# Expert weights in blocks of 1024 columns, down rows two to a partition, one low-part operation a load, and a fixed ring of five stages

## The chip, the cores and the metric

The kernel runs on one core of one Trainium2 chip. The metric is the device time of one execution in microseconds (us), the median of several runs. The engines are TensorE (PE; its weight loads are listed apart as PEld), VectorE (DVE), ScalarE (ACT), GpSimd (POOL) and SyncE (SP), whose queue issues the transfers from HBM.

## What is computed

A transformer with 256 tokens of 1024 features in float32: a first block of two layers (differential attention with a dense feed-forward, then a gated recurrence with a mixture of experts) and a second block of two layers (sparse attention with a gated MLP, a feed-forward with a short convolution, and a gated projection). The part that the change is about is the mixture of experts:

```python
logits = (t @ w_router).astype(F32)
top_val, top_idx = lax.top_k(logits, 2)                  # of 8 experts
combine = ...                                            # softmax of the two, by expert
for e in range(8):
    gt, up = jnp.split(t @ w_gate_up[e], 2, axis=-1)     # 1024 -> 2 * 3584
    y = (jax.nn.silu(gt) * up) @ w_down[e]               # 3584 -> 1024
    out = out + combine[:, e:e + 1] * y
```

The weights of the eight experts are 8 x 3 x 1024 x 3584 floats, 352 MB. Each is read once.

## The kernel before, in words

**Float32 products.** PE multiplies in a reduced format (float32r). Each operand is therefore split into a high part (a rounded copy, made by ACT, line 229) and a low part (the rest, a subtraction on DVE, line 230), and each product is three matmuls: high by high, low by high, high by low. Every weight tile of the program takes the same way: SP issues a load into a *stage* (`wload`, L217; pool `stp`, `N_STAGE` = 5 tiles of 128 x 2048 floats, 1 MB); ACT writes the high part and DVE the low part, in two halves of 128 x 1024 (`wsplit`, pools `whp` with `N_HI` = 6 halves and `wlp` with `N_LO` = 5); PE reads both; then stage and halves are free again. ACT and DVE work in order, so an instruction that waits holds up those behind it.

**Who sets the order.** The program is written with tile pools under `TileContext(nc, auto_bufs=True)`. A planner places the instructions of each engine at build time, by dependences, free buffers and its own estimates of cost. It may take a later instruction first, and it may raise the number of buffers of a pool where its walk gets stuck. On the chip each engine then follows its list. The order that the trace shows is therefore not always that of the source.

**The experts** (`moe`, `expert`, `run_experts`). The tokens of two experts at a time are gathered by matmul (`pair`), up to 128 tokens each; a branch handles the case of more than 128 and is not taken here. For each expert, seven groups of 512 hidden columns: `gate_up(g)` multiplies the tokens with the gate columns and the up columns (`pg`, `pu`, two PSUM banks of pool `pb`; four loads of 4 feature blocks x 512 columns, named `ste`, whose parts are `hie` and `loe`; 48 matmuls, L264 to L266), then ACT applies silu (L1137) and DVE multiplies (L1138), which gives `eh`. `down(g)` turns `eh` by four transposes (L1146), splits it (`hh` on ACT L283, `hl` on DVE L284) and multiplies with two loads of 256 rows of the down weights (`std`, with `hid` and `lod`; 24 matmuls of 512 columns, L1158 high by high, L1159 low by high, L1160 high by low), summed in two banks `y` over the seven groups. The loop runs `gate_up(g)` and then `down(g - 1)`. `scatter` brings `y` back to the tokens. One such round of 72 matmuls and six loads is called a *group* below, and the passage from the last matmul of `gate_up` to the first products of `down` a *turn*; there are 56 of each.

**The feed-forwards** (`swiglu_ff`, once in the first block, twice in the second) go through 11 *pairs* of 128 hidden columns: a gate tile `g` and an up tile `u` (8 feature blocks x 256 columns, `hig`/`log` and `hiu`/`lou`), 96 matmuls of 256 columns in the order of the feature blocks, so that both tiles are read to the end; then `down` of the pair before (a tile `dn`, 48 matmuls). DVE takes the sums out of PSUM (L640), ACT and DVE do the rest and split the result.

Of the kernel before, what the change touches and what calls it, by code (L numbers as in the profile page):

```python
# [10 lines left out]
F32 = mybir.dt.float32  # L11
# [11 lines left out]
N_AHEAD = (2, 0)  # L23
# [6 lines left out]
N_STAGE, N_HI, N_LO, N_G, N_T, N_S = 5, 6, 5, 30, 14, 64  # L30
# [64 lines left out]
# vectors over the features, as columns of 128: (key, how many columns)  # L95
# [15 lines left out]
def layout(v):  # L111
    """the arrays of the launch: the weights as they come, the rest laid out as the chip reads it"""
# [21 lines left out]
def body(ctx: ExitStack, tc: tile.TileContext, I, out, stop=None):  # L134
# [4 lines left out]
    stp = ctx.enter_context(tc.tile_pool(name="stp", bufs=N_STAGE))  # L139
# [27 lines left out]
    def S(n, s="s"):  # L167
        return sp.tile([128, 16 if n <= 16 else 64], F32, tag="s" if n <= 16 else "sw", name=nm(s), bufs=N_S if n <= 16 else 1)[:, :n]
# [16 lines left out]
    keep = {F32: cst.tile([128, 4096], F32, name="keep"), F32R: cst.tile([128, 512], F32R, name="keepr")}  # L185
# [12 lines left out]
    V.memset(onec, 1.0 / 1024)  # L198

# [7 lines left out]
    class Halves:  # L207
        def __init__(self, tiles, per):
            self.tiles, self.per = tiles, per

        def __getitem__(self, idx):
            _, k, sl = idx
            return self.tiles[k // self.per][:, k % self.per, sl]

    def wload(w, k0, kn, c0, width, s):
        st = stp.tile([128, 2048], F32, tag="st", name=nm("st" + s))
        nc.sync.dma_start(r3(st[:, :kn * width], kn),  # L217
                          w[k0 * 128:(k0 + kn) * 128, c0:c0 + width].rearrange("(k p) f -> p k f", p=128))
        return st, kn, kn * width, s

    def wsplit(loaded):
        st, kn, n, s = loaded
        his, los = [], []
        m = n // 2
        for q in range(2):
            hi = whp.tile([128, 1024], F32R, tag="hi", name=nm("hi" + s))
            lo = wlp.tile([128, 1024], F32R, tag="lo", name=nm("lo" + s))
            sq = st[:, q * m:q * m + m]
            A.activation(hi[:, :m], sq, AF.Copy)  # L229
            V.tensor_tensor(lo[:, :m], sq, hi.bitcast(F32)[:, :m], op=OP.subtract)  # L230
            his.append(r3(hi[:, :m], kn // 2))
            los.append(r3(lo[:, :m], kn // 2))
        return Halves(his, kn // 2), Halves(los, kn // 2)

    def wtile(w, k0, kn, c0, width, s):
        return wsplit(wload(w, k0, kn, c0, width, s))

# [8 lines left out]
    def wpieces(w, k0, kn, c0, width, s):  # L246
        """wtile in pieces of 512, which leaves its tiles to what is under way"""
        wh, wl = Pieces(), Pieces()
        for k in range(kn):
            for f in range(width // 512):  # L250
                st, hi, lo = G("st" + s), G2("hi" + s, F32R), G("lo" + s, F32R)
                nc.sync.dma_start(st, w[(k0 + k) * 128:(k0 + k) * 128 + 128, c0 + f * 512:c0 + f * 512 + 512])
                split(st, hi, lo, None)
                wh.tiles[k, f], wl.tiles[k, f] = hi, lo
        return wh, wl
# [74 lines left out]
    def squares(src, how):  # L330
        """tiles whose sum over features, through the matrix of ones, is the mean square"""
# [10 lines left out]
    def stats_r(src, how="later"):  # L342
        """1 / rms over the 1024 features, by token"""
# [13 lines left out]
    def rows_R(r, keep=True):  # L357
        """the same along the free dimension"""
# [48 lines left out]
    def feat_1024(X, w, s, order, side=None, hook=None):  # L407
        """X times w, by features; side yields what it makes of X while the rest is multiplied"""
# [67 lines left out]
    def steps(gen, n=None):  # L476
        """runs n steps of a generator (all of them without n); whether it goes on"""
# [42 lines left out]
    def by_R(lst, R, f=None, tile=G):  # L520
        """keeps a product by features, times R"""
# [9 lines left out]
    def by_r(lst, r, func=AF.Copy, tile=G):  # L531
        """keeps a product by tokens, times r"""
# [12 lines left out]
    def mem_attn(qmT, kmT, vm, XC):  # L545
        """attention over the memory (queries scaled), its output in pair 3 of XC"""
# [44 lines left out]
    def head_rms(po, extra, XC, hp, col):  # L591
        """rms norm of two heads by token and (times extra), then their transposes, split"""
# [398 lines left out]
    def moe(acc):  # L991
        # the first weights, before the branch
        ahead = []
        for n in range(N_AHEAD[0]):
            g, kh, b = n // 4, n // 2 % 2, n % 2
            ld = wload(I["moe_w_gate_up"][0, 0], kh * 4, 4, b * 3584 + g * 512, 512, "e")
            if n < N_AHEAD[1]:
                ahead.append(lambda hl=wsplit(ld): hl)
            else:
                ahead.append(lambda ld=ld: wsplit(ld))  # L1000
# [17 lines left out]
        # tokens by rows, split  # L1018
# [47 lines left out]
        # the rms of the tokens, and the weights of their two experts  # L1066
# [56 lines left out]
        def expert(e, X, j, SC, cw, first):  # L1123
            wgu, wd = I["moe_w_gate_up"][0, e], I["moe_w_down"][0, e]
            load = wtile if first else wpieces
            y = []

            def gate_up(g):
                pg, pu = PB("pg"), PB("pu")
                for kh in range(2):  # L1130
                    for ps, c0 in ((pg, g * 512), (pu, 3584 + g * 512)):
                        wh, wl = ahead.pop(0)() if ahead and first else load(wgu, kh * 4, 4, c0, 512, "e")
                        for k in range(4):
                            mm3t(ps, X, kh * 4 + k, j, wh[:, k, :], wl[:, k, :], kh == 0 and k == 0, kh == 1 and k == 3)
                t = G2("eh")
                rc = cw[:, 2 * j + 1:2 * j + 2]
                A.activation(t, pg, AF.Silu, scale=rc)  # L1137
                V.scalar_tensor_tensor(t, pu, rc, t, op0=OP.mult, op1=OP.mult)  # L1138
                return t

            def down(g, t):
                if g == 0:
                    y.extend([PA("y"), PA("y")])
                pt = PC("ht")
                for f in range(4):
                    T.transpose(pt[:, f * 128:f * 128 + 128], t[:, f * 128:f * 128 + 128], ident)  # L1146
                h, l = G2("hh", F32R), G2("hl", F32R)
                split(pt, h, l, None)
                for fp in range(2):
                    wh, wl = load(wd, g * 4 + fp * 2, 2, 0, 1024, "d")  # L1150
                    order = [(f, hf) for f in range(2) for hf in range(2)]
                    if g == 6 and fp == 1:
                        order = [(f, hf) for hf in range(2) for f in range(2)]
                    for f, hf in order:
                        fs = slice((fp * 2 + f) * 128, (fp * 2 + f) * 128 + 128)
                        a, b = wh[:, f, hf * 512:hf * 512 + 512], wl[:, f, hf * 512:hf * 512 + 512]
                        opens, ends = g == 0 and fp == 0 and f == 0, g == 6 and fp == 1 and f == 1
                        T.matmul(y[hf], lhsT=h[:, fs], rhs=a, start=opens, stop=False)  # L1158
                        T.matmul(y[hf], lhsT=l[:, fs], rhs=a, start=False, stop=False)  # L1159
                        T.matmul(y[hf], lhsT=h[:, fs], rhs=b, start=False, stop=ends)  # L1160
# [18 lines left out]
        def run_experts(slot, first):  # L1179
            ctxs = {0: pair(0, slot)}  # L1180
            prev = None
            fns = {}
            for e in range(8):
                for g in range(7):
# [5 lines left out]
                    if prev is not None:  # L1190
                        pe, pg, pt = prev
                        fns[pe][1](pg, pt)
                        if pg == 6:
                            fns[pe][2]()
                    prev = (e, g, t)
                    if first and e % 2 == 1 and g == 3 and e < 7:
                        ctxs[e // 2 + 1] = pair(e // 2 + 1, slot)
            fns[7][1](6, prev[2])
# [27 lines left out]
    def post(acc, gain, cols, fill):  # L1226
        """adds the normalized acc; the operand of the next products comes with it"""
# [18 lines left out]
    def proj(i, out):  # L1246
        """p @ w_ple_proj, features by rows, halved (the gate's own half lies in tanh)"""
# [19 lines left out]
    def gelu_gen(x, n):  # L1267
        """x (1 + tanh(...)) in place: twice the gelu"""
# [8 lines left out]
    def second_loads(i):  # L1277
        load_cols(I["cols2"][i], COLS_2, str(i), [("w2", 256)])
        if i == 0:
            k2 = cst.tile([128, sum(OFFS[n][1] for n in K2)], F32, name="k2")  # L1280
# [10 lines left out]
    def second(i, pj, fill, X):  # L1291
# [117 lines left out]
        # keys and values  # L1409
# [14 lines left out]
        # queries, their two parts side by side  # L1424
# [52 lines left out]
        gts = [sp.tile([128, 24], F32, tag="gates", name=nm("gates"), bufs=2) for _ in range(2)]  # L1477
# [90 lines left out]
        facs = [sp.tile([128, 24], F32, tag="fac", name=nm("fac"), bufs=2) for _ in range(2)]  # L1568

        def cmp_attn(c):  # L1570
            """over the compressed keys: opens at[c]"""
# [266 lines left out]
```

## Time and profile before

| | |
|---|---|
| median of 3 runs | 2308.17 us (2307.86 to 2312.56) |
| profiled execution, its own time | 2313.2 us, which is the span of the profile; nothing lies around it |
| instructions in it | 36939 |
| read from HBM | 547.70 MB |

The profile is of one execution, on the one core that is used. Busy time on PE is modelled: a matmul stays busy until its result has drained, so that neighbours overlap, and the pace of PE is read from the starts of its matmuls. PEclk is the granted clock of TensorE as a share of 2.4 GHz. A wait is put down to the instruction that released it.

### The profile page before, as it was taken

To read this page: it belongs to the slowest core of one execution; us is meant where nothing else is said; L and a number is where in the kernel's file an instruction comes from. 1 tells how busy PE (TensorE), PEld (TensorE's weight loads), DVE (VectorE), ACT (ScalarE), POOL (GpSimd) and SP (SyncE) were. 2 spreads that over 40 slices of the span, in tenths; PEclk is the share of its full clock that TensorE was granted. 3 is DMA by queue.
4 is the path that set the end of the run, shared out by engine and by line. 5 is a ranking of instruction groups with operands and counts; after the bars stand their busy time and mean duration, and the time that the engine had idled before them with its cause. 6 is when DMAs were issued, how large, how long until landed. Compare 5 with 4: busy or idle time off the path is not lost. (4 is left out here: it accounts for less than half of the span.)

```text
span 2313.2 us, 36939 instructions
## 1 busy us (share of the span) xinstructions
PE 2239.2 (97%) x14218; PEld 2019.2 (87%) x14218; DVE 1817.8 (79%) x2701; ACT 1474.7 (64%) x2138; POOL 76.4 (3%) x83
## 2 busy tenths in 40 slices
PE   8999999998999999999999999999999999989998
PEld 7889999997878888888888888879899998989998
DVE  6666576766888898989898989888777777867776
ACT  5554457435777777777777777777665565765554
POOL 0100001000000000000000000000000001000001
PEclk9999999998999999999999999999999999989998
DMA  8445556224999999999999999986245544525550
GB/s 288 139 137 174 195 171 204 92 78 167 359 348 335 349 353 372 338 354 351 373 350 341 349 378 350 372 299 221 74 136 193 182 147 137 186 78 183 183 178 19
DMA packets 297113, 551.23 MB, mean 238 GB/s; under 512 B 10336, under 2 KB 132064, under 8 KB 296928
## 3 DMA queue, kind: packets, MB, share of 16 engines
q1 hardware_dynamic: 296928, 548.78, 67.5%
q8 instruction: 114, 1.87, 0.3%
q14 instruction: 71, 0.58, 0.1%
HBM read 547.70 MB, written 1.05 MB: 237 GB/s over the span
## 5 line engine op out<-in xcount | busy, mean ns | idle before, releaser
L230 DVE TENSOR_TENSOR loe<-ste,hie 128x1024 fp32r<-128x1024 f32 x448 | 520.0, 1217 | 12.4 <-ACT hie L229 4.2
L229 ACT ACTIVATE hie<-ste 128x1024 fp32r<-128x1024 f32 x448 | 439.5, 1053 | 23.9 <-PE ac L260 9.9
L230 DVE TENSOR_TENSOR lod<-std,hid 128x1024 fp32r<-128x1024 f32 x224 | 264.9, 1218 | 17.1 <-ACT hid L229 15.6
L229 ACT ACTIVATE hid<-std 128x1024 fp32r<-128x1024 f32 x224 | 221.4, 1057 | 4.8 <-PE pg L265 2.3
L266 PE MATMUL pu<-loe,eh 128*128 128x512 f32 x448 | 176.7, 394 | 1.4 <-DVE loe L230 1.4
L1159 PE MATMUL y<-hid,hl 128*128 128x512 f32 x448 | 175.7, 392 | 2.0 <-DVE hl L284 2.0
L264 PE MATMUL pg<-hie,eh 128*128 128x512 f32 x448 | 175.4, 391 | 0.3 <-ACT eh L286 0.3
L266 PE MATMUL pg<-loe,eh 128*128 128x512 f32 x448 | 175.6, 392 | 0.0
L264 PE MATMUL pu<-hie,eh 128*128 128x512 f32 x448 | 174.7, 390 | 0.0
L265 PE MATMUL pg<-hie,el 128*128 128x512 f32 x448 | 174.6, 390 | 0.0
L265 PE MATMUL pu<-hie,el 128*128 128x512 f32 x448 | 174.6, 390 | 0.0
L1158 PE MATMUL y<-hid,hh 128*128 128x512 f32 x448 | 173.4, 392 | 0.7 <-ACT hh L283 0.7
L1137 ACT ACTIVATE eh<-pg,cw 128x512 f32<-128x512 f32 x56 | 38.6, 689 | 203.4 <-PE pg L266 203.4
L1160 PE MATMUL y<-lod,hh 128*128 128x512 f32 x448 | 163.4, 407 | 0.8
L258 PE MATMUL gu<-xh,hig 128*128 128x256 f32 x528 | 150.8, 286 | 3.7 <-ACT xh L286 3.7
L230 DVE TENSOR_TENSOR lou<-stu,hiu 128x1024 fp32r<-128x1024 f32 x66 | 80.4, 1220 | 91.1 <-PE gu L259 82.9
L259 PE MATMUL gu<-xh,log 128*128 128x256 f32 x528 | 150.5, 285 | 0.0
L260 PE MATMUL gu<-xl,hiu 128*128 128x256 f32 x528 | 150.5, 285 | 0.0
L258 PE MATMUL gu<-xh,hiu 128*128 128x256 f32 x528 | 150.4, 285 | 0.0
L259 PE MATMUL gu<-xh,lou 128*128 128x256 f32 x528 | 150.3, 285 | 0.0
L260 PE MATMUL gu<-xl,hig 128*128 128x256 f32 x528 | 150.1, 285 | 0.0
L258 PE MATMUL ac<-hh,hidn 128*128 128x256 f32 x528 | 149.4, 283 | 0.0
(516 smaller groups left out, 6279.5 us busy)
## 6 DMA issues: line engine op xcount, KB each, us to landing
ste<-in_moe_w_gate_up_dram SPq DMA_DIRECT2D x224, 1024.0 KB, 7.2
std<-in_moe_w_down_dram SPq DMA_DIRECT2D x112, 1024.0 KB, 5.5
stg<-in_w_up_dram SPq DMA_DIRECT2D x22, 1024.0 KB, 5.1
stu<-in_w_up_dram SPq DMA_DIRECT2D x22, 1024.0 KB, 5.1
stdn<-in_w_down_dram SPq DMA_DIRECT2D x22, 1024.0 KB, 4.8
stg<-in_dense_w_gate_up_dram SPq DMA_DIRECT2D x11, 1024.0 KB, 5.0
stu<-in_dense_w_gate_up_dram SPq DMA_DIRECT2D x11, 1024.0 KB, 5.0
stdn<-in_dense_w_down_dram SPq DMA_DIRECT2D x11, 1024.0 KB, 4.9
```

The source lines that it names most:

```text
L229: A.activation(hi[:, :m], sq, AF.Copy)
L230: V.tensor_tensor(lo[:, :m], sq, hi.bitcast(F32)[:, :m], op=OP.subtract)
L258: T.matmul(o, lhsT=lh, rhs=rh, start=start, stop=False, **kw)
L259: T.matmul(o, lhsT=ll, rhs=rh, start=False, stop=False, **kw)
L260: T.matmul(o, lhsT=lh, rhs=rl, start=False, stop=stop, **kw)
L264: T.matmul(o, lhsT=xh, rhs=wh, start=start, stop=False, **kw)
L265: T.matmul(o, lhsT=xl, rhs=wh, start=False, stop=False, **kw)
L266: T.matmul(o, lhsT=xh, rhs=wl, start=False, stop=stop, **kw)
L1137: A.activation(t, pg, AF.Silu, scale=rc)
L1158: T.matmul(y[hf], lhsT=h[:, fs], rhs=a, start=opens, stop=False)
L1159: T.matmul(y[hf], lhsT=l[:, fs], rhs=a, start=False, stop=False)
L1160: T.matmul(y[hf], lhsT=h[:, fs], rhs=b, start=False, stop=ends)
```

## The change

- **Gate and up** (`GW`): four blocks of 1024, 1024, 1024 and 512 hidden columns in place of seven groups of 512. A load of a wide block holds 2 feature blocks x 1024 columns (rows of 4 KB in place of 2 KB). `gate_up` now writes four banks of pool `pa` for a wide block, `y` moves to pool `pb`, and `down` of a wide block has four loads and eight transposes. The number of bytes, of loads (336) and of matmuls (4032) stays.
- **Down**: the load puts rows 2p and 2p + 1 in partition p, 8 KB in one piece; the transposes read every second column of `eh` to match.
- **Parts of an expert's tile** (`wrows`): high and low part are one tile of 2048 each; ACT still writes the high part in two halves, DVE writes the low part in one operation over 2048 columns, after both.
- **All other tiles** (`wsplit`): also one tile of 2048 for each part, written in halves by both engines as before. `N_HI`, `N_LO` = 3, 3 such tiles in place of 6 and 5 halves.
- **Stages**: slices of one array, taken in turn, always five, in place of a pool.
- The gathering of the next pair is called after block 1 of 4 (before, group 3 of 7). Some small tiles move to the array of constants. Comments are taken out.

```diff
-N_STAGE, N_HI, N_LO, N_G, N_T, N_S = 5, 6, 5, 30, 14, 64
+GW = (1024, 1024, 1024, 512)
+N_STAGE, N_HI, N_LO, N_G, N_T, N_S = 5, 3, 3, 30, 14, 64
...
+    ring = cst.tile([128, 2048 * N_STAGE], F32, name="st")
+    stages = [ring[:, n * 2048:n * 2048 + 2048] for n in range(N_STAGE)]
+
+    def stage():
+        stages.append(stages.pop(0))
+        return stages[-1]
+
+    def HL(s):
+        return (whp.tile([128, 2048], F32R, tag="hi", name=nm("hi" + s)),
+                wlp.tile([128, 2048], F32R, tag="lo", name=nm("lo" + s)))
...
     def wsplit(loaded):
         st, kn, n, s = loaded
-        his, los = [], []
         m = n // 2
+        hi, lo = HL(s)
         for q in range(2):
-            hi = whp.tile([128, 1024], F32R, tag="hi", name=nm("hi" + s))
-            lo = wlp.tile([128, 1024], F32R, tag="lo", name=nm("lo" + s))
-            sq = st[:, q * m:q * m + m]
-            A.activation(hi[:, :m], sq, AF.Copy)
-            V.tensor_tensor(lo[:, :m], sq, hi.bitcast(F32)[:, :m], op=OP.subtract)
+            sl = slice(q * m, q * m + m)
+            A.activation(hi[:, sl], st[:, sl], AF.Copy)
+            V.tensor_tensor(lo[:, sl], st[:, sl], hi.bitcast(F32)[:, sl], op=OP.subtract)
...
+    def wrows(w, r0, per, c0, width, s, loaded=None):
+        n = 2048 // width
+        if loaded is None:
+            st = stage()
+            pat = "(p k) f -> p k f" if per else "(k p) f -> p k f"
+            nc.sync.dma_start(r3(st, n), w[r0:r0 + 128 * n, c0:c0 + width].rearrange(pat, p=128))
+        else:
+            st = loaded[0]
+        hi, lo = HL(s)
+        for q in range(2):
+            A.activation(hi[:, q * 1024:q * 1024 + 1024], st[:, q * 1024:q * 1024 + 1024], AF.Copy)
+        V.tensor_tensor(lo, st, hi.bitcast(F32), op=OP.subtract)
+        return r3(hi, n), r3(lo, n)
...
             def gate_up(g):
-                pg, pu = PB("pg"), PB("pu")
-                for kh in range(2):
-                    for ps, c0 in ((pg, g * 512), (pu, 3584 + g * 512)):
-                        wh, wl = ahead.pop(0)() if ahead and first else load(wgu, kh * 4, 4, c0, 512, "e")
-                        for k in range(4):
-                            mm3t(ps, X, kh * 4 + k, j, wh[:, k, :], wl[:, k, :], kh == 0 and k == 0, kh == 1 and k == 3)
+                c0, width = g * gw[0], gw[g]
+                nb, n = width // 512, 2048 // width
+                pss = [[PA("gu") for _ in range(nb)] for _ in range(2)]
+                for k0 in range(0, 8, n):
+                    for b in range(2):
+                        for k, wh, wl in up_rows(k0, b * 3584 + c0, width):
+                            for hf in range(nb):
+                                cs = slice(hf * 512, hf * 512 + 512)
+                                mm3t(pss[b][hf], X, k, j, wh[:, cs], wl[:, cs], k == 0, k == 7)
...
-            def down(g, t):
+            def down(g, ts):
                 if g == 0:
-                    y.extend([PA("y"), PA("y")])
-                pt = PC("ht")
-                for f in range(4):
-                    T.transpose(pt[:, f * 128:f * 128 + 128], t[:, f * 128:f * 128 + 128], ident)
...
+                    y.extend([PB("y"), PB("y")])
+                for n, t in enumerate(ts):
+                    pt = PC("ht")
+                    for q in range(2):
+                        for f in range(2):
+                            src = r3(t[:, q * 256:q * 256 + 256], 128)[:, :, f]
+                            T.transpose(pt[:, (q * 2 + f) * 128:(q * 2 + f) * 128 + 128], src, ident)
```

## Rows read from the trace of the kernel before

**Rows 1.** Part 1 of the page: span, busy time and its share, by engine

```profile
span 2313.2 us, 36939 instructions
PE 2239.2 (97%) x14218; PEld 2019.2 (87%) x14218; DVE 1817.8 (79%) x2701; ACT 1474.7 (64%) x2138; POOL 76.4 (3%) x83
```

**Rows 2.** Windows: us, busy us (instructions) by engine, PEclk, DMA share, GB/s

```profile
545.00:1520.00 975.00, 969.16 (x4447) 791.03 (x4447) 868.22 (x844) 717.72 (x813) 0.00 (x0) 1.00 0.96 351
600.00:650.00 50.00, 49.98 (x227) 40.52 (x226) 44.89 (x42) 38.45 (x40) 0.00 (x0) 1.00 1.03 384
185.00:400.00 215.00, 213.93 (x1783) 213.56 (x1782) 140.54 (x179) 119.33 (x168) 5.53 (x3) 1.00 0.57 186
1710.00:1870.00 160.00, 160.00 (x1335) 160.00 (x1335) 123.58 (x195) 92.41 (x136) 0.00 (x0) 1.00 0.55 179
```

**Rows 3.** Timeline of PE over one group of an expert: start, us, instruction

```profile
905.96 0.39 PE L1158 MATMUL y<-hid,hh 128*128 128x512 f32 x1
...
906.87 0.73 PE L1160 MATMUL y<-lod,hh 128*128 128x512 f32 x2
...
908.37 0.60 PE L1146 MATMUL ht<-keep,eh 128*128 128x128 f32 x4
908.72 0.71 PE L1160 MATMUL y<-lod,hh 128*128 128x512 f32 x2
...
912.01 0.39 PE L264 MATMUL pg<-hie,eh 128*128 128x512 f32 x1
...
920.17 0.39 PE L264 MATMUL pu<-hie,eh 128*128 128x512 f32 x1
```

**Rows 4.** Waits of PE's weight loads, 547 to 1527 us: total, times, longest

```profile
PEld y L1160 <- DVE lod L230: 12.3, 39, 0.6
PEld pu L266 <- DVE loe L230: 3.9, 6, 0.7
PEld y L1159 <- DVE hl L284: 3.9, 6, 1.2
PEld ht L1146 <- DVE eh L1138: 1.9, 3, 0.7
PEld y L1158 <- ACT hh L283: 1.8, 5, 0.9
PEld sc L1172 <- ACT yh L286: 1.8, 6, 0.3
```

**Rows 5.** Timelines of ACT and of DVE over the same group

```profile
903.44 0.69 ACT L1137 ACTIVATE eh<-pg,cw 128x512 f32<-128x512 f32 x1 [4.41 <-PE pg L266]
904.02 0.59 ACT L283 ACTIVATE hh<-ht 128x512 fp32r<-128x512 f32 x1
904.50 3.90 ACT L229 ACTIVATE hid<-std 128x1024 fp32r<-128x1024 f32 x4
...
905.59 1.23 DVE L230 TENSOR_TENSOR lod<-std,hid 128x1024 fp32r<-128x1024 f32 x1 [0.25 <-ACT hid L229]
906.74 0.74 DVE L1138 SCALAR_TENSOR_TENSOR eh<-pu,cw,eh 128x512 f32<-128x512 f32 x1
...
910.80 9.16 DVE L230 TENSOR_TENSOR loe<-ste,hie 128x1024 fp32r<-128x1024 f32 x8
```

**Rows 6.** Transfers: SP's longest wait, and loads with median us to landing

```profile
SPq L217 <- DVE loe L230: 458.0, 212, 14.0
...
ste<-in_moe_w_gate_up_dram SPq DMA_DIRECT2D x224, 1024.0 KB, 7.2
std<-in_moe_w_down_dram SPq DMA_DIRECT2D x112, 1024.0 KB, 5.5
```

**Rows 7.** Timelines of PE and DVE where a feed-forward pair's gate and up end

```profile
243.68 0.28 PE L258 MATMUL ac<-hh,hidn 128*128 128x256 f32 x1
...
244.24 1.28 DVE L640 TENSOR_TENSOR ff<-gu,R 128x512 f32<-128x512 f32 x2
245.85 1.22 DVE L230 TENSOR_TENSOR lou<-stu,hiu 128x1024 fp32r<-128x1024 f32 x1
```

More of the change, by code (lines that the diff above doesn't have):

```diff
@@ L167, in S @@
     def S(n, s="s"):
-        return sp.tile([128, 16 if n <= 16 else 64], F32, tag="s" if n <= 16 else "sw", name=nm(s), bufs=N_S if n <= 16 else 1)[:, :n]
+        return C(n) if n > 16 else sp.tile([128, 16], F32, tag="s", name=nm(s))[:, :n]
     def PA(s="p"):
@@ L183, in bcast_rows @@
         return bass.AP(tensor=ap1d.tensor, offset=ap1d.offset, ap=[[0, 128], [1, n]])
-    keep = {F32: cst.tile([128, 4096], F32, name="keep"), F32R: cst.tile([128, 512], F32R, name="keepr")}
+    keep = {F32: cst.tile([128, 4176], F32, name="keep"), F32R: cst.tile([128, 640], F32R, name="keepr")}
     used = {F32: 0, F32R: 0}
@@ L991, in moe @@
     def moe(acc):
[L993 to L1000, printed above, removed]
+        ahead = [wload(I["moe_w_gate_up"][0, 0], 0, 2, b * 3584, 1024, "e") for b in range(2)]
         wr = S(64, "wr")
@@ L1141, in down @@
-            def down(g, t):
-                if g == 0:
-                    y.extend([PA("y"), PA("y")])
-                pt = PC("ht")
-                for f in range(4):
-                    T.transpose(pt[:, f * 128:f * 128 + 128], t[:, f * 128:f * 128 + 128], ident)
[L1147 to L1160, printed above, removed]
@@ new lines, in expert, with up_rows @@
+            gw = GW if first else (512,) * 7
+            def up_rows(k0, c0, width):
+                n = 2048 // width
+                if first:
+                    wh, wl = wrows(wgu, k0 * 128, 0, c0, width, "e", ahead.pop(0) if ahead else None)
+                    return [(k0 + k, wh[:, k, :], wl[:, k, :]) for k in range(n)]
+                wh, wl = wpieces(wgu, k0, n, c0, width, "e")
+                return [(k0 + k, Row(wh, k), Row(wl, k)) for k in range(n)]
+            def gate_up(g):
+                c0, width = g * gw[0], gw[g]
[7 more added lines that the diff above has]
+                                mm3t(pss[b][hf], X, k, j, wh[:, cs], wl[:, cs], k == 0, k == 7)
+                rc = cw[:, 2 * j + 1:2 * j + 2]
+                ts = []
+                for hf in range(nb):
+                    t = G2("eh")
+                    A.activation(t, pss[0][hf], AF.Silu, scale=rc)
+                    V.scalar_tensor_tensor(t, pss[1][hf], rc, t, op0=OP.mult, op1=OP.mult)
+                    ts.append(t)
+                return ts
@@ new lines, in down @@
+            def down(g, ts):
+                if g == 0:
+                    y.extend([PB("y"), PB("y")])
[5 more added lines that the diff above has]
+                            T.transpose(pt[:, (q * 2 + f) * 128:(q * 2 + f) * 128 + 128], src, ident)
+                    h, l = G2("hh", F32R), G2("hl", F32R)
+                    split(pt, h, l, None)
+                    for q in range(2):
+                        r0 = g * gw[0] + n * 512 + q * 256
+                        wh, wl = wrows(wd, r0, 2, 0, 1024, "d") if first else wpieces(wd, r0 // 128, 2, 0, 1024, "d", 2)
+                        opens, ends = r0 == 0, r0 == 3584 - 256
+                        order = [(f, hf) for f in range(2) for hf in range(2)]
+                        if ends:
+                            order = [(f, hf) for hf in range(2) for f in range(2)]
+                        for f, hf in order:
+                            fs = slice((q * 2 + f) * 128, (q * 2 + f) * 128 + 128)
+                            a, b = wh[:, f, hf * 512:hf * 512 + 512], wl[:, f, hf * 512:hf * 512 + 512]
+                            T.matmul(y[hf], lhsT=h[:, fs], rhs=a, start=opens and f == 0, stop=False)
+                            T.matmul(y[hf], lhsT=l[:, fs], rhs=a, start=False, stop=False)
+                            T.matmul(y[hf], lhsT=h[:, fs], rhs=b, start=False, stop=ends and f == 1)
@@ L1182, in run_experts @@
             fns = {}
+            last = len(GW) - 1 if first else 6
             for e in range(8):
-                for g in range(7):
+                for g in range(last + 1):
                     if g == 0:
@@ L1192, in run_experts @@
                         fns[pe][1](pg, pt)
-                        if pg == 6:
+                        if pg == last:
                             fns[pe][2]()
                     prev = (e, g, t)
-                    if first and e % 2 == 1 and g == 3 and e < 7:
+                    if first and e % 2 == 1 and g == 1 and e < 7:
                         ctxs[e // 2 + 1] = pair(e // 2 + 1, slot)
-            fns[7][1](6, prev[2])
+            fns[7][1](last, prev[2])
             fns[7][2]()
@@ L1279, in second_loads @@
         if i == 0:
-            k2 = cst.tile([128, sum(OFFS[n][1] for n in K2)], F32, name="k2")
+            k2 = C(sum(OFFS[n][1] for n in K2))
             o = 0
@@ L1475, in second @@
                 kT[kg].append(k)
-        gts = [sp.tile([128, 24], F32, tag="gates", name=nm("gates"), bufs=2) for _ in range(2)]
+        gts = shared.setdefault("gates", None) or [C(24) for _ in range(2)]
+        shared["gates"] = gts
         us = [G("u") for _ in range(2)]
@@ L1567, in second @@
         at = [G("at") for _ in range(2)]
-        facs = [sp.tile([128, 24], F32, tag="fac", name=nm("fac"), bufs=2) for _ in range(2)]
         def cmp_attn(c):
```

32 lines of the change are left out of this document (13 added, 19 removed).

## The prediction

> **What bounds the kernel now.** I read the page's busy times first, then windows by stage, the timeline of PE inside one group, the waits, and the transfers. By the page PE is busy for 97% of the span, DVE for 79%, ACT for 64% [rows 1]; since PE's busy time is modelled, that is a hint and no proof. The windows give the stages: the experts take 545 to 1520 us and a little more, and there all three are near their ends, PE 969 of 975 us, DVE 868, and the DMA share is 0.96. In the feed-forwards PE is full, DVE at 0.65 (first block) and 0.77 (second), DMA at 0.55 [rows 2].
>
> The pace of PE shows that it is the bound among the experts. From 912.01 to 920.17 us lie 36 matmuls of 512 columns: 8.16 / 36 = 0.2267 us each. Four transposes take 908.72 - 908.37 = 0.35 us. A group of 72 matmuls and four transposes cannot go below 16.32 + 0.35 = 16.67 us. From 905.96 to 920.17 are 60 matmuls and the four transposes, 13.95 us by that pace, and 14.21 us passed [rows 3]: 0.26 us of a group was waiting. That is all a change of tiles can win there; the number of matmuls stays. The waits of PE's weight loads say where it lies: at the turns, above all before the first low part of a down tile, and in sum 12.3 + 3.9 + 3.9 + 1.9 + 1.8 + 1.8 = 25.6 us over the stage [rows 4], or 0.46 us for each of the 56 turns.
>
> The turn itself is seen on ACT and DVE [rows 5]. Call the first product of `down` T (905.96). ACT, in order, has waited 4.41 us for the gate sum; silu starts at T - 2.52, the split of `hh` at T - 1.94, the four `hid` halves from T - 1.46, one every 0.975 us. The first `lod` runs from T - 0.37 to T + 0.86; PE, after four products that need only the high part, takes it at T + 0.91 [rows 3]. So the chain gate sum, silu, `hh`, `hid`, `lod` is just in time.
>
> Transfers do not bind: SP waited 458 us for DVE to free a stage after a `loe` [rows 6], so a stage waits for its reader.
>
> **The change part by part.**
>
> *Fewer turns.* Eight experts by four blocks make 32 turns in place of 56. At 0.46 us each that is 14.6 in place of 25.6 us: -11.0 us.
>
> *What a turn costs afterwards.* The low part of 2048 columns can start only after both high halves, and it is longer. No row has such an operation; two back to back take 2 x 1.145 us (eight in 9.16 [rows 5]), so I take 2.3 us. The first of the two silus can start 0.68 us earlier (three matmuls of the other 512 columns follow its sum), so ACT still reaches the first `hid` half at T - 1.46 and ends the second at T + 0.57. The low part then ends at T + 2.9, or at T + 3.2 if both products of L1138 (0.74 us each, the second ready at about T + 0.2) are placed ahead of it. PE has eight products with the high part alone until T + 1.81 and eight transposes of 0.09 us until T + 2.5; the high half of the next tile is ready at about T + 1.5, worth 0.9 us more. Today's list already fills holes so: the transposes stand in the middle of `down`, and the products with `hid` go ahead of those with `lod` [rows 3]. So the wait before the first low part is between 0 (the next tile's products are placed ahead) and 3.2 - 1.81 = 1.4 us (nothing is). I keep today's sum of 0.46 us a turn, which lies between. At 0 for all waits the stage wins 25.6 us. At 1.4, with the others' (25.6 - 12.3) / 56 = 0.24, it is 1.64 x 32 = 52.5 us: 27 us lost.
>
> *DVE's time.* 672 low parts become 336. Each of those left out saves between nothing and the 0.085 us by which a single one (1.23) exceeds the pace (1.145) [rows 5]: 0 to 29 us of DVE, all of it under PE's products (868 of 975 us [rows 2]). Priced 0; it makes recovery after a turn easier. After the turn DVE needs 2.3 us for a tile and PE 12 x 0.2267 = 2.72, so a lead grows by 0.4 us a tile.
>
> *Transfers.* Gate and up rows go from 2 to 4 KB, the size that the down loads have now, which land in 5.5 us against 7.2 [rows 6]. Under a stage that is freed later than it is wanted this is worth nothing: 0. The ring of five: a stage is held for landing (5.5 to 7.2 us), two high halves (2.0) and the low part (2.3), 9.8 to 11.5 us, and is wanted again after five loads of (16.67 + 0.26) / 6 = 2.82 us, 14.1 us. The cover is 2.6 us or more: 0. If it is gone, up to a microsecond at each turn, 32 us.
>
> *Transposes of every second column.* No row has a strided one. Between nothing and as much again as now, 224 x 0.0875 = 20 us. I take 0: they stand in the hole of the turn.
>
> *The gather of the next pair* comes after block 1, which ends at hidden column 2048, as group 3 does now: 0. The loads ahead of the routing are two before and after: 0.
>
> *The feed-forwards*, 33 pairs without a gap on PE: 1783 instructions in 215 us, 0.12 us each [rows 2]. Now a half of a gate or up tile comes free when PE is half through. With parts of one tile the slots of both tiles come free only at the end E of the pair's 96 products (243.68 [rows 7]), and the next pair starts 48 x 0.12 = 5.76 us later. What it needs first is the first half of `g` and of `u`: on DVE, from 0.56 us after E, the two L640 (1.28) and two low halves (2.3), which end at E + 4.1 if the planner takes them first. Margin 1.6 us, so 0. If it takes the rest of the activation first (some four operations on 256 columns, at 1.28 / 4 = 0.32 us each by L640's pace, and in the second block 0.12 x 17.3 = 2.0 us more, by the busy shares [rows 2]), the half comes at E + 5.4 or E + 7.4: 1.7 x 22 = 37 us lost. Three tiles are as many halves as today's six, and one more for the low parts, so the attention stages stay as they are, give or take 5 us.
>
> **Sum.** -11 us on the execution profiled, 2313.2 to 2302. The median of the runs shown is 5.0 us below that execution; carried over, **2297 us**.
>
> **The rivals.**
>
> *The low part is late at each turn* (slower). The mechanism of the second item: the list on PE puts the four low products of a down tile directly behind its eight high ones, L1138 goes ahead on DVE, and each turn costs 1.64 us: +27, 2335 us. For it: the first `lod` is in time by 0.05 us now, and the new one comes some 2 us later. Against it: PE has 0.9 us more to do without it, and the list fills holes. It decides above 25.6 / 32 = 0.8 us a turn. Chance 0.17.
>
> *The feed-forward waits for whole tiles* (slower): up to +37 on the forecast: 2334 us. For it: DVE idles until PE frees buffers even now, and `lou` follows at 245.85 behind both L640 [rows 7]. Against it: the margin of 1.6 us, and other stages' work can wait 11.5 us longer than these halves. It decides where they are ready later than E + 5.76. Chance 0.10.
>
> *No change*: the stage is bound by its transfers as much as by PE, so that nothing won at turns is kept. The mean is 351 GB/s at a DMA share of 0.96; if that is the ceiling, the stage stays as long as it is: 2308 us. Against it: a window at 384 GB/s, at the same row sizes [rows 2], and SP's wait for stages. The same result comes where savings and losses at turns cancel. Chance 0.20. The Trainium skill (DMA: Bandwidth & Descriptors, "Specifications") puts the limit of one core's HBM at about 358 GB/s; by that figure the 352 MB of the experts need 984 us, an estimate, and the windows give them 975 us and a little more, which speaks for this rival. The trace does not agree: 384 GB/s was moved in the window from 600 to 650 us.
>
> **How the numbers follow.** The forecast, a gain between 5 and 26 us at the turns, has a chance of 0.50 and its own range is 2283 to 2303 us. 0.03 is left for gains or losses elsewhere. A measurement of this kernel can tell about 0.2%, 4.6 us. Faster: 0.52; within: 0.20; slower: 0.28. The range runs from 2283, where all waits vanish, into the late low part, to 2322 us; outside are the larger part of that rival and the feed-forward's, some 0.2.
>
> **What the profile afterwards would show.** The span of the experts falls by some 11 us at a pace of PE that stays 0.2267. PE's wait for `lod` comes about 32 times and in sum below 12 us; above 25 us the first rival holds. The low part of 2048 columns takes 2.3 us, DVE's busy time among the experts falls, gate and up loads land in about 5.5 us, and the DMA share falls with the rate up or the same. In the feed-forwards PE starts a matmul every 0.12 us without gaps between pairs; weight loads there that wait for `log` or `lou` would show the second rival. I am wrong if PE waits for a load, if transposes are longer, or if attention stages change by more than 5 us.

## The result, and the profile after

The changed kernel takes 2373.95 us (median; 2367.78 to 2377.54), 1.0274 times the time before, with an interval of 1.0258 to 1.029: 2.7% slower. Forecast were 2297 us, with a range to 2322. The profiled execution spans 2372.2 us against 2313.2 [rows 1]. The page's first part:

```profile
span 2372.2 us, 35922 instructions
PE 2257.4 (95%) x14218; PEld 2037.2 (86%) x14218; DVE 1782.4 (75%) x2366; ACT 1470.5 (62%) x2138; POOL 74.8 (3%) x83
```

DVE has 335 instructions and 35 us less to do, 24 us of it in the low parts of the experts' loads (784.9 to 760.6), and PE's share has fallen: it waits more. The windows (columns as in [rows 2]) tell in which stage:

```profile
545.00:1520.00 975.00, 928.80 (x4165) 761.83 (x4163) 793.26 (x482) 681.08 (x761) 0.00 (x0) 0.98 0.89 331
200.00:300.00 100.00, 100.00 (x836) 100.00 (x835) 57.17 (x72) 42.88 (x60) 0.00 (x0) 1.00 0.53 176
1800.00:1950.00 150.00, 150.00 (x1252) 150.00 (x1252) 111.66 (x178) 82.08 (x125) 0.00 (x0) 1.00 0.57 187
```

In the same 975 us among the experts PE gets through 282 matmuls fewer, and its granted clock is 0.98 there, not 1.00. The feed-forwards run on at a matmul every 0.12 us. From the first gate product to the last down product of the experts it is 1062.1 us, before 993.1: that is +69.0, and all the rest of the program is 10.0 us shorter in these two executions.

The waits of PE's weight loads among the experts (560 to 1600 us: total, times, longest) name the culprits:

```profile
PEld y L1198 <- DVE lod L250: 34.0, 16, 3.0
PEld y L1197 <- DVE hl L310: 30.4, 24, 2.3
PEld gu L290 <- ACT hie L249: 2.1, 4, 0.6
PEld y L1196 <- ACT hh L309: 2.0, 8, 0.4
```

Before, `lod` stood there with 12.3 us and `hl` with 3.9, the longest 0.6 and 1.2 us [rows 4]. Now there are single waits of 2 to 3 us, for the low part of the weights and, as much, for the low part of the hidden block. Two turns show how they come about. The first is a turn whose `down` is of a wide block; PE, ACT and DVE:

```profile
854.33 0.72 PE L1196 MATMUL y<-hid,hh 128*128 128x512 f32 x2
856.92 0.50 PE L1197 MATMUL y<-hid,hl 128*128 128x512 f32 x1 [1.87 <-DVE hl L310]
857.26 0.47 PE L1198 MATMUL y<-lod,hh 128*128 128x512 f32 x1
857.53 0.63 PE L1197 MATMUL y<-hid,hl 128*128 128x512 f32 x1
857.96 0.63 PE L1198 MATMUL y<-lod,hh 128*128 128x512 f32 x1
858.38 0.63 PE L1196 MATMUL y<-hid,hh 128*128 128x512 f32 x1
...
860.52 0.55 PE L1198 MATMUL y<-lod,hh 128*128 128x512 f32 x1
...
853.68 0.60 ACT L309 ACTIVATE hh<-ht 128x512 fp32r<-128x512 f32 x1
...
852.62 1.44 DVE L1171 SCALAR_TENSOR_TENSOR eh<-gu,cw,eh 128x512 f32<-128x512 f32 x2 [4.43 <-PE gu L292]
853.98 2.28 DVE L250 TENSOR_TENSOR lod<-st,hid 128x2048 fp32r<-128x2048 f32 x1
856.18 0.69 DVE L310 TENSOR_TENSOR hl<-ht,hh 128x512 fp32r<-128x512 f32 x1
```

`hh` is ready at 854.28, but DVE has begun the low part of 2048 columns at 853.98, and `hl` stands behind it until 856.18. PE has two products to do without `hl` and then stands. The second is a later turn, whose `down` is of a narrow block:

```profile
951.09 0.39 PE L1196 MATMUL y<-hid,hh 128*128 128x512 f32 x1
...
952.17 0.39 PE L1197 MATMUL y<-hid,hl 128*128 128x512 f32 x1
955.11 0.74 PE L1198 MATMUL y<-lod,hh 128*128 128x512 f32 x2 [2.55 <-DVE lod L250]
...
948.71 1.05 ACT L249 ACTIVATE hid<-st 128x1024 fp32r<-128x1024 f32 x1
949.65 0.68 ACT L1170 ACTIVATE eh<-gu,cw 128x512 f32<-128x512 f32 x1
950.22 0.60 ACT L309 ACTIVATE hh<-ht 128x512 fp32r<-128x512 f32 x1
950.70 2.95 ACT L249 ACTIVATE hid<-st 128x1024 fp32r<-128x1024 f32 x3
...
950.86 0.69 DVE L310 TENSOR_TENSOR hl<-ht,hh 128x512 fp32r<-128x512 f32 x1 [5.15 <-ACT hh L309]
951.46 1.40 DVE L1171 SCALAR_TENSOR_TENSOR eh<-gu,cw,eh 128x512 f32<-128x512 f32 x2
952.78 4.49 DVE L250 TENSOR_TENSOR lod<-st,hid 128x2048 fp32r<-128x2048 f32 x2
```

DVE stands idle until 950.86, though the first half of `hid` is ready at 949.76: the one low operation needs the second half too, which ACT writes only behind the second silu and `hh`, from 950.70 to about 951.7. Then it goes behind `hl` and both products of L1171, and ends at 955.06. PE has four products with `hid`, not eight, ahead of it on its list.

These two turns stand for most of the loss. In the expert stage 26 steps from one start on PE to the next are above 1.2 us: seven of 2.94 to 2.95 us ahead of the first `lod` of a narrow block, eight of 1.53 to 1.74 ahead of the first `lod` of a wide one, and eleven of 1.87 to 2.26 ahead of an `hl` product of a wide one. At no turn does PE have more than four products ahead of its first low one.

The stops have a sequel. In windows over the first of these turns PE's granted clock (the third number from the end) falls after the wait:

```profile
854.00:857.00 3.00, 1.13 (x8) 0.70 (x6) 3.00 (x4) 3.00 (x5) 0.00 (x0) 1.00 0.08 33
857.00:858.00 1.00, 1.00 (x4) 0.78 (x5) 1.00 (x1) 1.00 (x2) 0.00 (x0) 0.72 0.70 74
858.00:861.00 3.00, 3.00 (x9) 2.35 (x8) 3.00 (x3) 1.73 (x3) 0.00 (x0) 0.53 0.94 358
```

From 857.53 to 860.52 the eight products start 2.99 / 7 = 0.427 us apart in place of 0.2267: the 1.2 GHz level. The Trainium skill (TensorE: Matmul & The Clock Gate, "Wait — 56ns, not 53.3ns?") gives 426.7 ns from start to start for 512 columns at that level; the trace agrees.

The loads among the experts (median us from issue to landing; [rows 6] has 7.2 and 5.5):

```profile
st<-in_moe_w_gate_up_dram SPq DMA_DIRECT2D x224, 1024.0 KB, 6.2
st<-in_moe_w_down_dram SPq DMA_DIRECT2D x112, 1024.0 KB, 6.8
```

### The profile page after: what moved, and what is told of

It is laid out like the page before. It is cut to its first block, busy times and chain, and to the rows that moved or that the text cites. A ratio compares the mean times of both kernels' runs of the same rounds, so it can differ in the third digit from the quotient of the medians.

```text
span 2372.2 us, 35922 instructions
## 1 busy us (share of the span) xinstructions
PE 2257.4 (95%) x14218; PEld 2037.2 (86%) x14218; DVE 1782.4 (75%) x2366; ACT 1470.5 (62%) x2138; POOL 74.8 (3%) x83
## 4 chain that ended last, share of the span: by engine, by line
PE 63%; DVE 6%; issue 3%; ACT 3%; DMA 2%; POOL 0%; DVEq 0%; POOLq 0%; SPq 0%; ACTq 0%
PE gu L290 7%; PE gu L292 7%; PE gu L291 7%; PE y L1198 5%; PE y L1197 4%; PE y L1196 4%; PE gu L286 4%; PE gu L285 4%; PE gu L284 4%; PE ac L286 2%; PE ac L284 2%; PE ac L285 2%; DVE lod L250 2%; DMA st<-in_moe_w_down_dram 2%; PE tw L290 1%
## 5 line engine op out<-in xcount | busy, mean ns | idle before, releaser
L250 DVE TENSOR_TENSOR loe<-st,hie 128x2048 fp32r<-128x2048 f32 x224 | 507.7, 2290 | 58.3 <-PE gu L292 23.9
L249 ACT ACTIVATE hie<-st 128x1024 fp32r<-128x1024 f32 x448 | 446.9, 1055 | 131.8 <-DMA st<-in_moe_w_gate_up_dram 44.2
L290 PE MATMUL gu<-hie,eh 128*128 128x512 f32 x896 | 350.6, 391 | 0.9 <-ACT hie L249 0.6
L291 PE MATMUL gu<-hie,el 128*128 128x512 f32 x896 | 349.5, 390 | 0.0
L292 PE MATMUL gu<-loe,eh 128*128 128x512 f32 x896 | 338.2, 391 | 0.0
L250 DVE TENSOR_TENSOR lod<-st,hid 128x2048 fp32r<-128x2048 f32 x112 | 252.9, 2286 | 11.0 <-ACT hid L249 3.6
L249 ACT ACTIVATE hid<-st 128x1024 fp32r<-128x1024 f32 x224 | 222.9, 1060 | 10.6 <-PE gu L291 8.5
L290 PEld LDWEIGHTS gu<-hie,eh 128*128 128x128 f32 x896 | 168.4, 188 | 37.0 <-ACT hie L249 2.1
L291 PEld LDWEIGHTS gu<-hie,el 128*128 128x128 f32 x896 | 168.3, 188 | 34.0
L292 PEld LDWEIGHTS gu<-loe,eh 128*128 128x128 f32 x896 | 167.8, 188 | 33.4
```

Source lines behind the costliest of these rows:

```text
L249: A.activation(hi[:, q * 1024:q * 1024 + 1024], st[:, q * 1024:q * 1024 + 1024], AF.Copy)
L250: V.tensor_tensor(lo, st, hi.bitcast(F32), op=OP.subtract)
L290: T.matmul(o, lhsT=xh, rhs=wh, start=start, stop=False, **kw)
L291: T.matmul(o, lhsT=xl, rhs=wh, start=False, stop=False, **kw)
L292: T.matmul(o, lhsT=xh, rhs=wl, start=False, stop=stop, **kw)
```

## The experiments

Each kernel was timed against the kernel before on one chip. That kernel's median was 2308.0 us beside the changed one and 2311 us beside the others, so compare the ratios.

| kernel | us | ratio, interval |
|---|---|---|
| changed | 2374.0 | 1.0274, 1.0258 to 1.0290 |
| a_lo2: changed, low parts in halves | 2315.4 | 1.0024, 1.0013 to 1.0035 |
| a_lo2d: halves for down alone | 2318.4 | 1.0034, 1.0020 to 1.0048 |
| a_lo2e: halves for gate and up alone | 2366.1 | 1.0238, 1.0220 to 1.0256 |
| a_hh: changed, hidden block split early | 2347.1 | 1.0156, 1.0132 to 1.0181 |
| a_hh_lo2: both | 2321.7 | 1.0040, 1.0026 to 1.0054 |
| a_512: changed, blocks of 512 | 2357.3 | 1.0199, 1.0177 to 1.0222 |
| a_512_lo2: and halves | 2300.8 | 0.9963, 0.9953 to 0.9974 |
| a_512_hh: and early split | 2300.6 | 0.9954, 0.9936 to 0.9972 |
| a_512_f1: a_512_lo2, first down half cut again | 2301.3 | 0.9962, 0.9945 to 0.9979 |
| b_ring: before, ring of five | 2306.3 | 0.9976, 0.9960 to 0.9992 |
| b_ring_lo1: and one low operation | 2356.6 | 1.0204, 1.0185 to 1.0223 |
| b_ring_d4: b_ring, down's low parts in four | 2334.6 | 1.0104, 1.0084 to 1.0124 |

The second table is worked out from the start times of PE's matmuls in each profile, from the first gate product to the last down product. Whatever a start comes later than the pace (0.2267 us after a matmul of 512 columns, 0.12 after 256, 0.11 after 128) is put to the instruction that was late; steps of 0.41 to 0.44 us, the pace at a granted clock of 0.5, have a column of their own. Steps late by less than 0.03 us are left out, so the columns explain a difference between stages to within some 4 us. Only in the changed kernel, a_lo2e and a_hh does the granted clock fall with such steps; the 0.2 to 1.2 us of three other rows are steps of that length at a clock of 1.00.

| us | stage | late for `lod` | for `hl` or `hh` | half clock | else |
|---|---|---|---|---|---|
| before | 993.1 | 9.8 | 4.1 | 0.2 | 9.6 |
| changed | 1062.1 | 35.7 | 31.4 | 16.6 | 6.0 |
| a_lo2 | 1007.3 | 22.2 | 8.2 | 0 | 5.4 |
| a_lo2d | 1007.9 | 6.5 | 9.6 | 1.2 | 17.5 |
| a_lo2e | 1058.7 | 40.0 | 25.1 | 14.4 | 4.9 |
| a_hh | 1036.4 | 46.2 | 8.9 | 1.4 | 8.0 |
| a_hh_lo2 | 1007.0 | 22.0 | 2.2 | 0 | 10.5 |
| a_512 | 1046.0 | 47.0 | 5.9 | 0 | 22.7 |
| a_512_lo2 | 993.1 | 10.4 | 1.0 | 0 | 11.2 |
| a_512_hh | 989.0 | 0.1 | 4.7 | 0 | 11.0 |
| a_512_f1 | 993.6 | 7.3 | 6.1 | 0 | 11.4 |
| b_ring | 991.8 | 10.7 | 1.2 | 0 | 10.3 |
| b_ring_lo1 | 1045.1 | 47.3 | 6.1 | 0.4 | 22.4 |
| b_ring_d4 | 1016.0 | 0.6 | 9.9 | 0 | 37.9 |

The theory: the turns of the experts (A), by the one low operation, the wide block, or both. The rivals: five fixed stages make data late (B), or the layout and the coarse tiles do (C).

**Low parts in halves (a_lo2).**

```diff
-        V.tensor_tensor(lo, st, hi.bitcast(F32), op=OP.subtract)
+        for q in range(2):
+            sl = slice(q * 1024, q * 1024 + 1024)
+            V.tensor_tensor(lo[:, sl], st[:, sl], hi.bitcast(F32)[:, sl], op=OP.subtract)
```

> The changed kernel with the low part of each expert load in two operations of 1024 columns instead of one of 2048. Theory A (the turns: PE waits at each of the 32 turns for hl and for the first lod; in the changed kernel PE lost 41.3 us ahead of the low products and 42.4 us ahead of the hl products): the first low half ends one half, about 1.1 us, earlier at each turn, so the loss ahead of the low products falls by about 32 x 1.1 = 35 us, that ahead of hl stays: about 2339 us. Theory B (the data come late, five fixed stages): nothing at the turns hangs on the cut, 2374 us within 5. Theory C (the coarse tiles or the two-row layout): also 2374.

It came down by 58.5 us, 24 more than theory A gave, and in other parts: the wait for `lod` fell by 13.5 us by the table and not by 35, that for `hl`, which was to stay, by 23.2, and the half clock was gone (16.6). B and C, which gave no change, fall as main causes.

**Blocks of 512 (a_512), and the ring (b_ring) and the one operation (b_ring_lo1) on the kernel before.**

a_512 (the next pair is gathered after block 3 again), then the ring, then the one operation:

```diff
-GW = (1024, 1024, 1024, 512)
+GW = (512,) * 7
...
-        st = stp.tile([128, 2048], F32, tag="st", name=nm("st" + s))
+        st = stage()
...
-            V.tensor_tensor(lo[:, :m], sq, hi.bitcast(F32)[:, :m], op=OP.subtract)
...
+            V.tensor_tensor(lo[:, :n], st[:, :n], hi.bitcast(F32)[:, :n], op=OP.subtract)
```

> The changed kernel with gate and up in seven blocks of 512 columns (56 turns), all else as changed: one low operation a load, two-row down loads, ring of five. Theory A1 (the block of 1024 makes hl late: two silus, a half split and two products of gate and up stand ahead of it): hl is late by no more than before, the loss per turn falls from 2.8 us towards 0.5 to 1.6, at 56 turns 2312 to 2374 us with the low part as the rest. Theory A2 (the one low operation of 2.29 us is the cause alone): the low products wait some 1.3 us at 56 turns in place of 32, 73 us against 41: 2374 or more. Theory B (five fixed stages, late data): 2374, as the loads are as many and as large.

> The kernel before with the fixed ring of five stages in place of its pool of stages, alone. Theory B (the ring makes loads late): slower, towards 2374 if it is the whole cause. Theory A (the turns): 2308 us within 5, as no turn holds another order of work.

> The kernel before with the ring of five and hi and lo in whole tiles of 2048 columns, the low part of each expert load in one operation; blocks of 512 and the rows of the down loads as before. Theory A2 (the one low operation makes the first lod late by about half of its 2.29 us at each turn): 56 x 1.1 = about 60 us, 2368. Theory A1 (the wide block makes hl and lod late): at most some 10 us, 2308 to 2318. Theory C (row layout, wide block's data): 2308.

The ring alone is 0.24% faster; B is false. One low operation on top of it costs 1.0204 - 0.9976 = 2.3%, with blocks, rows and transposes as they were: 2357 us, 11 below what A2 gave and 39 above A1. (This kernel has the high and low parts in whole tiles too, which the lines above leave out; a_512_lo2 below has them with the low parts in halves and is no slower than b_ring, so they are not the cost.) a_512 is at the same 2357, inside A1's wide range and 17 below the least that A2 gave. So two rows in a partition and strided transposes cost nothing that shows (C is false), 17 us of the changed kernel's time go with its wide block, and A1 and A2 both hold in part. A turn of each, PE, ACT and DVE. First b_ring:

```profile
867.91 0.39 PE L1164 MATMUL y<-hid,hh 128*128 128x512 f32 x1
...
868.59 0.39 PE L1165 MATMUL y<-hid,hl 128*128 128x512 f32 x1
868.83 0.50 PE L1166 MATMUL y<-lod,hh 128*128 128x512 f32 x1
...
866.46 2.95 ACT L235 ACTIVATE hid<-st 128x1024 fp32r<-128x1024 f32 x3
...
867.55 1.23 DVE L236 TENSOR_TENSOR lod<-st,hid 128x1024 fp32r<-128x1024 f32 x1 [0.26 <-ACT hid L235]
```

The half ends at 868.78 and PE, four products after its first, takes it at 868.83. There is no slack. Now b_ring_lo1:

```profile
881.46 0.39 PE L1165 MATMUL y<-hid,hh 128*128 128x512 f32 x1
...
882.14 0.39 PE L1166 MATMUL y<-hid,hl 128*128 128x512 f32 x1
883.67 0.73 PE L1167 MATMUL y<-lod,hh 128*128 128x512 f32 x2 [1.14 <-DVE lod L239]
...
880.24 2.95 ACT L235 ACTIVATE hid<-st 128x1024 fp32r<-128x1024 f32 x3
...
881.33 2.29 DVE L239 TENSOR_TENSOR lod<-st,hid 128x2048 fp32r<-128x2048 f32 x1 [0.25 <-ACT hid L235]
```

The operation begins 0.13 us ahead of PE's first `down` product (881.46), not 0.36 as in b_ring (867.91), and is 1.06 us longer: together 1.29, and the start at 883.67 is 1.30 us behind the pace. In both turns PE has the same four products ahead of it, so here the one operation alone makes the difference. That by 56 would be 73 us; at some turns it is less, and the table has 47.3 - 10.7 = 36.6 for `lod`, and 12 more in the last column.

**Which of the low operations (a_lo2d, a_lo2e).** The edit of a_lo2 for the loads of down alone, or of gate and up alone ("a2lo2e" in the text below is a_lo2e).

> The changed kernel with the low part in halves for the down loads alone; gate and up keep one operation of 2048. Known by now: halves everywhere give 2315 us, one operation 2374. Theory A2a (only the down tile's own low operation counts, because the first y<-lod product needs it at once): about 2315 to 2320. Theory A2b (it is the loe operation of 2.29 us that stands ahead of hl and lod on DVE in program order): about 2374, and a2lo2e is the fast one.

> The changed kernel with the low part in halves for the gate and up loads alone; down loads keep one operation of 2048. Theory A2a: about 2365 to 2374, the y<-lod wait stays near 41 us. Theory A2b: about 2315. Both half right: each of the two between 2335 and 2355.

Halves for down alone bring 2.40 of the 2.50%, for gate and up alone 0.36. It is the operation whose result PE is standing at that counts, not DVE's work as a whole.

**What the block of 1024 costs (a_512_lo2).**

```diff
-GW = (1024, 1024, 1024, 512)
+GW = (512,) * 7
...
+            V.tensor_tensor(lo[:, sl], st[:, sl], hi.bitcast(F32)[:, sl], op=OP.subtract)
```

> The changed kernel with blocks of 512 and the low part in halves: what is left of the change is the ring, the whole tiles and the two-row down loads. Theory A (turns): as the kernel before with the ring, 2306 us within 4, and the difference to 2315 of the changed kernel in halves is what the block of 1024 costs. Theory C (row layout or coarse tiles): above 2315.

2300.8 us, 0.4% below the kernel before as well: with the low part in halves the wide block costs 1.0024 - 0.9963 = 0.6%, or 14 us. The stages say the same, 1007.3 against 993.1 us. In a_lo2 the turns whose `down` is of a narrow block are still late by some 1.65 us each ahead of `lod`.

**Smaller still (b_ring_d4, a_512_f1).** Down's low part in operations of 512 columns; in a_512_f1 only the first half of the first down load of a turn.

```diff
-            V.tensor_tensor(lo[:, :m], sq, hi.bitcast(F32)[:, :m], op=OP.subtract)
+            step = 512 if s == "d" else m
+            for o in range(0, m, step):
+                V.tensor_tensor(lo[:, o:o + step], sq[:, o:o + step], hi.bitcast(F32)[:, o:o + step], op=OP.subtract)
```

> The kernel before with the ring, and the low part of each down load in four operations of 512 columns instead of two of 1024. Theory A2 (PE waits at a turn for the end of the first low operation): the 10.7 us that PE still loses ahead of the low products fall to 3 or less, 2296 to 2301 us. Rival (what is late is the first high part or the load, not the length of the low operation): no change, 2306, or a few us slower by 112 x 2 more instructions on DVE.

> Blocks of 512, low parts in halves, but the first half of the first down load of each turn in two operations of 512 (56 instructions more). Theory A2 (PE waits for the first low operation): the 10.4 us lost ahead of lod fall to 2 or less, 2292 us. Rival from the kernel with four operations on every down load (2335 us; the wait ahead of lod went, but 24.7 us were lost at the first loe product of gate behind the turn): the order shifts likewise, 2305 to 2335.

The first was a miss. The late `lod` did go, from 10.7 to 0.6 us, but the kernel is 28 us slower than with the ring alone. Its waits (560 to 1550 us):

```profile
PEld pg L274 <- DVE loe L238: 34.6, 44, 1.3
PEld y L1168 <- DVE lod L238: 10.6, 52, 0.3
```

Now PE waits at the first low product of *gate* behind the turn. DVE's groups in the same stretch (busy us, mean ns, then idle time before them and what ended it), first b_ring_d4, then b_ring:

```profile
L238 DVE TENSOR_TENSOR loe<-st,hie 128x1024 fp32r<-128x1024 f32 x432 | 500.4, 1218 | 34.2 <-ACT hie L235 27.8 <-issue 3.0 <-ACT yh L294 2.3
L238 DVE TENSOR_TENSOR lod<-st,hid 128x512 fp32r<-128x512 f32 x439 | 274.0, 684 | 17.8 <-ACT hid L235 17.5
...
L236 DVE TENSOR_TENSOR loe<-st,hie 128x1024 fp32r<-128x1024 f32 x432 | 499.8, 1220 | 7.0 <-ACT hie L235 4.5 <-PE y L1166 1.1 <-issue 0.2
L236 DVE TENSOR_TENSOR lod<-st,hid 128x1024 fp32r<-128x1024 f32 x224 | 264.6, 1220 | 17.9 <-ACT hid L235 16.8
```

The smaller operations cost DVE only 14.9 us over all 112 loads (279.5 against 264.6; the window above holds 439 of the 448). What is new is that it stands idle ahead of `loe` until ACT has ended a high half, 27.8 us in place of 4.5; 16 of the stops of PE, 1.31 us from start to start, follow such an idle time of some 1.04 us. This points to the order of the lists, which differ, more than to the length; no run separates the two. Cut only where PE stands, in a_512_f1, the wait for `lod` fell from 10.4 to 7.3 us and that for `hl` rose from 1.0 to 6.1: no gain, and neither the 2292 us of A2 nor the 2305 to 2335 of its rival.

**The hidden block split early (a_hh, a_hh_lo2, a_512_hh).** Transposes and split move from `down` to the end of `gate_up`, a block ahead of their use.

```diff
             def gate_up(g):
...
-                return ts
+                hs = []
+                for t in ts:
+                    pt = PC("ht")
...
+                    split(pt, h, l, None)
+                    hs.append((h, l))
+                return hs
```

> The changed kernel (blocks of 1024, one low operation of 2048) with the transposes and the split of a hidden block written right behind its gate and up, one block ahead of its down products, so that hh and hl are ready a block early. Known: one low operation on the down loads costs 59 us, of which PE lost some 41 us ahead of lod and 42 us ahead of the hl and hh products. Theory H1 (hl is a wait of its own, from the split being late): the hl loss goes, 2330 to 2340 us. Theory H2 (the hl loss is the same lateness of DVE and of the order, it moves to the low products): 2365 to 2380.

> The same early split, with the low parts in halves. H1: what is left of the hl loss in the kernel with halves (8 us) goes, 2305 to 2310. H2: 2315 as without it; an early hh and hl also hold buffers a block longer, which would show as late loads: 2315 to 2325.

> Blocks of 512, low parts in halves, and the early split. Without the early split 2301 us, with 10.4 us lost ahead of lod and 1 us ahead of hl. H1 and H2 agree that there is little hl loss to win: 2299 to 2303; if DVE is freed of hl at the turn, the first lod comes 0.2 us earlier at 56 turns, 2290 to 2295.

With the one low operation it brings 27 us: the loss ahead of `hl` and `hh` falls by 22.5 and the half clock by 15.2, while that ahead of `lod` grows by 10.5 and the last column by 2.0, which leaves 25.2 of the 25.7 us by which the stage is shorter. H1 was right about `hl` and 7 us too good about the time; what H2 said, that the loss moves to the low products, holds for those 10.5 us. The wait that is left (a_hh):

```profile
PEld y L1201 <- DVE lod L250: 46.5, 41, 1.6
PEld y L1199 <- ACT hid L249: 12.6, 18, 0.8
```

With halves it brings nothing: 2321.7 against 2315.4 us with blocks of 1024, 2300.6 against 2300.8 with 512, though there the loss ahead of `lod` is 0.1 us. With blocks of 1024 H1 was too good by some 12 us; the stage is as long as without the early split, 1007.0 against 1007.3 us.

## Why the prediction was wrong

- *The bound and its pace*: right. PE sets the time of the experts, at 0.2267 us for a product.
- *Fewer turns, -11.0 us*: this is 24 turns at today's price, and stands or falls with the next step.
- *What a turn costs afterwards*: **the step that failed.** The waits were bounded by 1.64 us a turn and taken at 0.46. Measured are (35.7 + 31.4 + 16.6 + 6.0) / 32 = 2.8 us. Three things in it were wrong. First, "the list fills holes": PE's list has the low products behind four high ones at most, where eight and the next tile's were counted on; four is also what the kernel before has [rows 3]. Second, the waits other than that for `lod` were left at 0.24 us a turn, 7.7 us in all; they are 37.4, because the long operation on DVE holds up `hl`, which was never followed as work queued behind it. Third, the clock's fall after stops of 2 to 3 us, 16.6 us, was in no term. The part for `lod` itself stayed within its bound in sum, 35.7 us of 1.4 x 32 = 44.8, but not turn by turn, so that is luck: it is 2.8 us or more at seven narrow turns (the eighth narrow block stands at the very end, right behind another `down`), 1.6 to 1.7 at eight wide ones, and 0.2 or less at the others, where `hl` was the later one.
- *The length of the low operation, 2.3 us*: right, 2.29. *DVE's time*: the low parts of the experts take 24 us less, inside the 0 to 29 given, and that is worth nothing: right.
- *Transfers*: ring and row sizes cost nothing: right, and the ring alone gains 0.24%. Gate and up land in 6.2 us, between the 5.5 forecast and the 7.2 before; a_512_lo2, with rows of 2 KB as before, has 7.3. That the DMA share falls to 0.89 is a result, and so is the rate, which was to stay or rise and fell from 351 to 331 GB/s: at 854 to 857 us the share is 0.08, because DVE ends no low part and so frees no stage between 848.20 and 856.26, and SP issues its next load at 856.30.
- *Transposes*: near 0, right, though they are longer. Their weight loads take 207 ns (median), before 139, and in a row they start 0.12 us apart, before 0.11: an estimate from these steps is 3 us at most over 224. *Feed-forwards*: 0, right.
- *Attention stages within 5 us*: outside the experts the two profiled executions differ by 10.0 us (1320.1 and 1310.1). This is not shown to be a gain of the change. a_lo2 and a_lo2d differ from the changed kernel in the experts' low parts alone, and have 1303.9 and 1300.7 us there; and the profiled execution of the kernel before is 5.0 us above its median. The mean granted clock up to the experts goes along: 0.96 before, 0.97 in the changed kernel, 0.98 in a_lo2d. Why it differs was not followed.
- *The rivals*: the first, the late low part, was right in place and sign, and its sign in the profile came (34.0 us for `lod`, above 25). It gave 2335, 39 us short, for the reasons above. The feed-forward's rival and that of no change are false.

In sum, by the ratios, taken off in this order: one low operation a load +2.5% (58 us), the block of 1024 +0.6% (14), all else -0.37% (8.5). The planner orders every one of these kernels anew, so each figure holds the length of an operation together with the order that came with it; only the turn of b_ring and b_ring_lo1 above has them apart.

## What to carry to other kernels

Where an engine takes a result within a tenth of a microsecond of its making, as PE took `lod`, the length of the operation that makes it is on the critical path: merging two operations saved time on the engine that has room (24 us on DVE here) and cost more at such places (58 us). Look at every instruction that the longer one stands ahead of on its engine, not only at those that read its result. If both are wanted, merge only where no engine stands waiting (a_lo2d keeps the one operation for gate and up, and is within 3 us of a_lo2), and measure: the finer cut of all down tiles came out 28 us slower.

## What the runs showed of the hardware

Of the 26 steps above 1.2 us in the changed kernel's expert stage, 12 (1.99 to 2.95 us) were followed by five to eight products at a granted clock of 0.5; others of the same length (2.26, 2.95 us) had no such sequel. In b_ring_lo1, with 30 such steps of 1.31 to 1.53 us, the clock stayed at 1.00; in a_hh, with 20 of 1.23 to 1.73 us, it fell once.

Alone, one subtraction takes 0.68 us for 512 columns, 1.22 for 1024 and 2.29 for 2048. In a row the next begins before the last has ended: they start 0.60, 1.14 and 2.21 us apart. So 2048 columns in one operation save 0.06 us of DVE's time against two of 1024, and not the 0.15 by which the two durations exceed the one.

A transpose that reads every second column has a weight load of 207 ns (median; 196 in a_512), one of columns that lie together 139.
